# Second layer's MLP in two token groups of 512, and attention of tiles 2 and 3 beside the input projection

## The chip, the core and the metric

The kernel runs on one core of a Trainium2 chip. The metric is the time of one execution in device microseconds (us). The kernel before took 3335.85 us (median of three runs, 3335.21 to 3341.36). The engines: TensorE (PE, matrix products; its weight loads are shown as PEld), VectorE (DVE), ScalarE (ACT), GpSimd (POOL), and SyncE (SP), whose queue issues the DMA transfers here.

## What is computed

A backbone of two layers over 1024 latent tokens and 256 context tokens, each of width 1024. The essential lines of the reference, for one layer and the latent tokens (`h` is the normed and modulated input):

```python
a_z, bq, bk, bv, cq, ck, cv = split_proj(h @ w_in[i])
out_a = chunk_gmlp(a_z, a_ws[i], a_bs[i])                    # chunks of 128 tokens
out_b = window_attn_latent(q_b, k_b, v_b, k_bc, v_bc, b_sink[i])   # window +-128, 8 heads
o_c = diff_attn_latent(q_c, k_c, v_c, k_cc, v_cc, lam)       # 4 heads, two softmax maps, all keys
x = x + g1 * (jnp.concatenate([out_a, out_b, out_c], axis=-1) @ w_out[i])
x = x + g2 * conv_ffn(modulate(rms_norm(x, norm2_g[i]), sh2, sc2),
                      w_up[i], conv_w[i], conv_b[i], w_down[i])
```

`conv_ffn` multiplies by `w_up` (1024 x 5632), convolves each channel over three neighbouring tokens, gates (silu) and multiplies by `w_down` (2816 x 1024). The context tokens pass the first layer in the same way and serve only as keys and values in the second. The output is the latent stream.

## The kernel before

Tokens are worked in tiles of 128: tiles 0 to 7 are latent, 8 and 9 context. All products by weights are made in three terms: `wunit` (L111) loads a block of weights, ScalarE copies its high part (L115) and VectorE or GpSimd subtracts to get the low part (L109), and `mm3` (L123) issues three matmuls for each 128 x 128 block (L130 with the weights stationary, L132 with the tokens stationary).

A layer has these pieces:

- `norms` and `ipset`: norm of each tile, then the input projection in four column blocks, 3 to 0 (`inproj`, L422, matmuls on L132, 512 columns wide). Blocks 3 and 2 hold keys and values and the queries of attention C, block 1 the queries of attention B, block 0 the chunked gating. Results go to scratch memory in DRAM.
- `attn_c(L, hd, groups)` (L785): attention C for one head, over a list of tile pairs. A unit is one head and one pair: it loads the queries; the keys (Kc, L666) and values are loaded once for the head, with the first pair. Scores (L692), maxima on VectorE (L496), exponentials on ScalarE (L695), a combination of both maps on VectorE (L702), transposes (L727), the product with the values (L718), and a short chain that ends with two stores (L775).
- `attn_b(L, tiles)` (L782): attention B for one pair, in two units (one for each key/value head). It ends with four stores a unit (L640).
- `prep(L, G, ...)` (L804): the output projection for the tokens of a group `G` (loads of attention's results, oT, L799; matmuls on L130 that read oT), then the norms of the group's tiles. All columns of the projection, and so all tiles of the group, must be there before the norms.
- `mlp(L, G, ...)` (L840): 22 up steps `up(f)` of two weight blocks each, with the convolution on ScalarE and VectorE (L860 to L867), and down steps `down` after every four or three up steps. A `hook(f)` is called in the middle of up step f; with it the next group's `prep` is placed into the current group's MLP. The numbers in `HK` (L21) say at which step; the loads of oT are issued over the four steps ahead of it.
- `finish(L, G, ...)` (L908): in the second layer it transposes the result (L921) and stores the output.

A group is a run of tokens that share one pass over the MLP's weights: every group loads, splits and multiplies by all of `w_out`, `w_up` and `w_down`. The convolution needs one neighbour on each side, so a group keeps two columns of the one before it. A group's matmuls are as wide as one entry of its `segs` (256, 384, 386, 258 columns); a group with two segments multiplies both by a weight block while it is loaded, but its last down step passes over the weights once for each segment. The first layer has groups of 384 (with the context), 384 and 512 tokens. The second has 256 (tiles 0 and 1), 384 (tiles 2 to 4) and 384 (tiles 5 to 7), L946 to L951.

The engines' instruction order is not the program's order. A planner lays all instructions out by readiness in its own timeline and gives precedence to what stands earlier in the program; so the order of the calls sets precedence, and independent pieces are interleaved. Each engine then runs its list in order, as does SP's queue. What limits interleaving are the buffers of the tile pools. Attention's pool `at` has three key buffers, four for score rows (tag e), three for transposed rows, one for values and one for B's queries, and PSUM has one accumulator O for both attentions. `wide(True)` lets the weight products use two more PSUM banks (zS beside z); while attention runs, it is off.

The order of the second layer's part in question (L1179 to L1223): projection blocks 3 and 2; attention C of pair (0,1) over four heads; block 1; attention B of (0,1); block 0; then, with the projection's pools released, attention B of (2,3) and (4,5); attention C of both; `prep` of group a; attention B and C of (6,7); MLP of group a, with `prep` of group b at step 20; MLP of group b with `prep` of group c at step 12; `wide(True)`; MLP of group c. The `at` pool is released after group a's MLP.

Of the kernel before, what the change touches and what calls it, by code (L numbers as in the profile page):

```python
# [17 lines left out]
DRAM = bass.MemoryType.DRAM  # L18


HK = (16, 13, 20, 12)  # L21

WD = ("dddd", "dddd", "dddd", "dddd")

# [28 lines left out]
def trunk(ctx: ExitStack, tc: tile.TileContext, a: dict):  # L53
    nc = tc.nc
    act, dve, pool, pe, sp = nc.scalar, nc.vector, nc.gpsimd, nc.tensor, nc.sync

    def mkpool(name, bufs, side="left", space=None):
        kw = {"space": space} if space is not None else {}
        return tc.alloc_tile_pool(name=name, bufs=bufs, side=side, reuse_waits="tile", **kw)
# [28 lines left out]
    st = {"wd": 0}  # L88
    wb = {"zs": 4, "sq": 3, "kn": 3, "st": 2}
    xh = const.tile([P, KT], F32, name="xh")  # L90
# [691 lines left out]
    def attn_b(L, tiles, at, mkS, mkT, mkO):  # L782
        attend(units_b(L, tiles, at, mkS, mkT, mkO))

    def attn_c(L, hd, groups, at, mkS, mkT, mkO):  # L785
        attend(units_c(L, hd, groups, at, mkS, mkT, mkO))
# [17 lines left out]
    def prep(L, G, p, mp, pl=None, lo=dve):  # L804

        wd = G["W"]
        xg, oT, loads = pl or prep_loads(L, G, p)
        while loads:
            loads.pop(0)()
        if G["xh"]:  # L810
            dve.tensor_copy(xg[:, :, 0], xh)
        for (xc, n, pieces) in G["op"]:
            for ct in range(KT):
                w = wunit(a["w_out"][L][:, ct * P:ct * P + P], KT, P, eng=lo)
                ps = mkz()
                mm3(ps[:, :n], lambda j, k: w[:, j, k, :], lambda j, k: oT[:, j, k, xc:xc + n], KT)
                for (tok, o, m, s) in pieces:
                    xs = xg[:, ct, xc + o:xc + o + m]
                    sp.dma_start(out=xs, in_=x_s[:, ct, tok:tok + m])
                    dve.scalar_tensor_tensor(out=xs, in0=ps[:, o:o + m], scalar=mods[:, L, 16 + ct, s:s + 1], in1=xs,  # L820
                                             op0=ALU.mult, op1=ALU.add)
        hT = p.tile([P, 2, KT, wd], F32R, tag="h", name="h2", bufs=1)
        if G["xh"]:
            dve.tensor_copy(hT[:, :, :, 0:2], hal.bitcast(F32))
        big = lambda: mp.tile([P, KT, P], F32, name="nb", tag="nb", bufs=2)
        for i, (xc, hc, s) in enumerate(G["norm"]):
            norm_tile(L, 1, xg[:, :, xc:xc + P], s, hT[:, 0, :, hc:hc + P], hT[:, 1, :, hc:hc + P], mkU, big,
                      add=AN[L])

        def halo():  # L830
            if G["halo"] is not None:
                hc, xc = G["halo"]
                dve.tensor_copy(hal, hT[:, :, :, hc:hc + 2].bitcast(F32))
                dve.tensor_copy(xh, xg[:, :, xc])

        return xg, hT, halo
# [71 lines left out]
    def finish(L, G, xg, mp):  # L908
        if L < DEPTH - 1:
            for ct in range(KT):  # L910
                for (tok, xc, n) in G["out"]:
                    sp.dma_start(out=x_s[:, ct, tok:tok + n], in_=xg[:, ct, xc:xc + n])
            return
        for (tok, xc, n) in G["out"]:
            for o in range(0, n, P):
                m = min(P, n - o)
                ot = mp.tile([P, KT, P], F32, name="ot", tag="nb", bufs=2)
                for g in range(2):
                    px = mkT()
                    for k in range(4):  # L920
                        pe.transpose(px[:m, k * P:k * P + P], xg[:, 4 * g + k, xc + o:xc + o + m], ident)  # L921
                    if g:
                        dve.tensor_copy(ot[:m, 4:8], px[:m].rearrange("p (k t) -> p k t", k=4))
                    else:
                        act.activation(out=ot[:m, 0:4], in_=px[:m].rearrange("p (k t) -> p k t", k=4), func=AF.Copy)
                m16 = m - m % 16
                for r0, r1 in ((0, m16), (m16, m)):
                    if r1 > r0:
                        sp.dma_start(out=a["out"][0, tok + o + r0:tok + o + r1, :],
                                     in_=ot[r0:r1].rearrange("p k t -> p (k t)"))  # L930
# [5 lines left out]
    nrm = lambda n: [(1 + 128 * k, 2 + 128 * k, 0) for k in range(n)]  # L936
    G0 = [dict(id="a", xh=False, W=384, op=[(0, 384, [(0, 0, 128, 0), (SEQ, 128, 256, 1)])],
               norm=[(0, 0, 0), (128, 128, 1), (256, 256, 1)], halo=(126, 127),
# [4 lines left out]
          dict(id="c", xh=True, W=514, op=[(1, 512, [(512, 0, 512, 0)])], norm=nrm(4), halo=None,  # L943
               segs=[(0, 258, [(0, 258, 1, 257, 0, 0)]), (256, 258, [(0, 258, 1, 258, 256, 0)])],
               out=[(511, 0, 513)])]
    G1 = [dict(id="a", xh=False, W=256, op=[(0, 256, [(0, 0, 256, 0)])], norm=[(0, 0, 0), (128, 128, 0)],  # L946
               halo=(254, 255), segs=[(0, 256, [(0, 256, 0, 255, 0, 0)])], out=[(0, 0, 255)]),
          dict(id="b", xh=True, W=386, op=[(1, 384, [(256, 0, 384, 0)])], norm=nrm(3), halo=(384, 384),
               segs=[(0, 386, [(0, 386, 1, 385, 0, 0)])], out=[(255, 0, 384)]),
          dict(id="c", xh=True, W=386, op=[(1, 384, [(640, 0, 384, 0)])], norm=nrm(3), halo=None,  # L950
               segs=[(0, 386, [(0, 386, 1, 386, 0, 0)])], out=[(639, 0, 385)])]  # L951
    A1 = [[(2, 3), (4, 5)], [(6, 7)]]


    psA = mkpool("psA", 1, "right", PSUM)
# [15 lines left out]
    def wide(on):  # L971
        zc[1] = on
# [121 lines left out]
    def ahead(L, G, p, f, at_f, key):  # L1094
        if f == at_f - 4:
            st["pl"] = prep_loads(L, G, p)
        if at_f - 4 <= f < at_f:
            st["pl"][2].pop(0)()
        if f == at_f:
            st[key] = prep(L, G, p, M, st["pl"])  # L1100
# [8 lines left out]
    def hook(f):  # L1109
        ahead(0, G0[1], X2, f, HK[0], "x2")  # L1110

# [67 lines left out]
    ipset(1, be, (3, 2), w=w)  # L1179
    wide(False)  # L1180
    for hd in range(4):
        attn_c(1, hd, [(0, 1)], at, mkS, mkT, mkO)
    ipset(1, al[2:] + be, (1,))
    attn_b(1, (0, 1), at, mkS, mkT, mkO)
    ipset(1, al[2:] + be, (0,))
    hp2.release()
    wx.release()
# [1 line left out]
    nwk.release()  # L1189
    hp.release()  # L1190
    M = mkpool("M2", 2, "right")
    X2 = mkpool("X5", 1, "right")
    X1 = mkpool("X4", 1, "right")
    for t in A1[0]:
        attn_b(1, t, at, mkS, mkT, mkO)
    for hd in range(4):
        attn_c(1, hd, A1[0], at, mkS, mkT, mkO)
    x1 = prep(1, G1[0], X1, M)
    for t in A1[1]:
        attn_b(1, t, at, mkS, mkT, mkO)  # L1200
    for hd in range(4):
        attn_c(1, hd, A1[1], at, mkS, mkT, mkO)

    def hook(f):
        ahead(1, G1[1], X2, f, HK[2], "x2")

    mlp(1, G1[0], *x1, M, hook, pool)
    finish(1, G1[0], x1[0], M)
    X1.release()
    at.release()  # L1210
    X3 = mkpool("X6", 1, "left")

    def hook(f):
        ahead(1, G1[2], X3, f, HK[3], "x3")

    mlp(1, G1[1], *st["x2"], M, hook, pool)
    finish(1, G1[1], st["x2"][0], M)
    wide(True)
    mlp(1, G1[2], *st["x3"], M)
    finish(1, G1[2], st["x3"][0], M)  # L1220
    X3.release()
    X2.release()
    M.release()  # L1223
    psD.release()
    psT.release()
# [50 lines left out]
```

## Time and profile before

| what | value |
|---|---|
| time, median of three runs | 3335.85 us (3335.21 to 3341.36) |
| the profiled execution's own time | 3333.47 us |
| its span, first to last instruction | 3331.7 us |
| mean granted clock of TensorE | 0.977 |
| second layer's input projection, last matmul (L132) | 2131.8 us into the span |
| group a: first MLP matmul | 2286.5 us |
| group c: first matmul of the output projection | 2853.6 us |
| last up matmul of the last group | 3307.9 us |

Times within the profile are microseconds from the start of the span, and durations of one instruction are in nanoseconds (ns). A row that groups instructions names the line, engine, operation, the tiles written and read, the shape and the count; behind the bar stand busy time in us, the mean of one instruction in ns, and the idle time of the engine in front of them with what ended it. A row on one line of the kernel has the least, middle and greatest duration, and the first and last start. PEclk is the share of full speed that TensorE was granted.

### The profile page before, as it was taken

Reading aid. Unit: us, or ns where it says so; the run is one execution under the profiler, and the core shown is the slowest. Engines: PE = TensorE matmul, PEld = TensorE weight load, DVE = VectorE, ACT = ScalarE, POOL = GpSimd, SP = SyncE. Lnnn points to the kernel's source line nnn. Section 1 sums busy time; section 2 is a strip of 40 time slices with the busy share of each in tenths; the row PEclk is TensorE's granted clock in tenths of the full one; section 3 lists DMA queues with packets and bytes.
Section 4 is the critical chain, followed back from the end, with each engine's and each line's share of the span. In section 5 each row is a group of like instructions: output and inputs, shape, how many; then the busy total and the mean of one; then the engine's idle time right before and its main releaser. Section 6 shows DMA issues by size and latency. Waiting matters only on the chain.

```text
span 3331.7 us, 54585 instructions
## 1 busy us (share of the span) xinstructions
PE 3152.4 (95%) x19503; PEld 2750.3 (83%) x19503; DVE 2333.3 (70%) x5306; ACT 1744.9 (52%) x3059; POOL 887.0 (27%) x1170
## 2 busy tenths in 40 slices
PE   6999989899999999999999899999999999999999
PEld 3777556787998898998999777766887789999998
DVE  4776756766878785878777678647786685666666
ACT  3555645555556663656444345556665564444443
POOL 1545311223223550138001154222322323222000
PEclk8999989899999999999999999999999999999999
DMA  8655787245442853378343555445555446434433
GB/s 262 194 157 161 227 247 188 81 125 128 128 122 80 258 166 115 101 209 239 88 117 112 161 149 160 143 125 140 161 139 153 123 120 196 122 105 137 136 113 109
DMA packets 754127, 499.52 MB, mean 150 GB/s; under 512 B 81480, under 2 KB 697792, under 8 KB 753856
## 3 DMA queue, kind: packets, MB, share of 16 engines
q1 hardware_dynamic: 753856, 496.03, 52.1%
q8 instruction: 155, 2.54, 0.3%
q14 instruction: 116, 0.95, 0.1%
HBM read 432.48 MB, written 63.44 MB: 149 GB/s over the span
## 4 chain that ended last, share of the span: by engine, by line
PE 70%; DVE 10%; DMA 6%; ACT 3%; issue 3%; POOL 2%; SPq 1%; ACTq 0%; DVEq 0%; POOLq 0%
PE z L130 34%; PE zS L130 11%; PE z L132 7%; PE O L718 3%; PE O L619 3%; PE T L609 2%; PE T L727 2%; DVE wsp L109 2%; PE S L692 2%; DMA raw<-in_w_up_dram 1%; PE zS L132 1%; DVE ec L496 1%; POOL mev L171 1%; DMA mraw<-in_w_ada_dram 1%; DMA raw<-in_w_down_dram 1%
## 5 line engine op out<-in xcount | busy, mean ns | idle before, releaser
L130 PE MATMUL z<-h,wsp 128*128 128x386 f32 (+3 forms) x5280 | 872.9, 319 | 19.8 <-DVE t L867 5.8
L130 PEld LDWEIGHTS z<-h,wsp 128*128 128x128 f32 x5280 | 822.7, 190 | 36.0 <-issue 7.8
L115 ACT ACTIVATE wsp<-raw 128x1024 fp32r<-128x1024 f32 (+2 forms) x660 | 555.9, 845 | 426.9 <-PE z L130 183.8
L109 DVE TENSOR_TENSOR wsp<-raw,wsp 128x1024 fp32r<-128x1024 f32 (+2 forms) x516 | 561.9, 1091 | 104.3 <-ACT wsp L115 101.1
L130 PE MATMUL z<-g,wsp 128*128 128x386 f32 (+3 forms) x2640 | 460.9, 321 | 22.0 <-ACT wsp L115 7.1
L130 PEld LDWEIGHTS z<-g,wsp 128*128 128x128 f32 x2640 | 415.2, 190 | 38.6 <-issue 11.8
L132 PE MATMUL z<-wsp,h 128*128 128x512 f32 x1584 | 405.8, 402 | 14.2 <-ACT h L233 4.8
L109 POOL TENSOR_TENSOR wsp<-raw,wsp 128x128 fp32r<-128x128 f32 x528 | 252.8, 511 | 478.5 <-ACT wsp L115 379.9
L132 PEld LDWEIGHTS z<-wsp,h 128*128 128x128 f32 x1584 | 292.0, 191 | 80.7 <-ACT h L233 5.8
L130 PE MATMUL zS<-h,wsp 128*128 128x386 f32 (+1 forms) x2112 | 332.8, 313 | 5.5 <-DVE t L867 2.4
L130 PEld LDWEIGHTS zS<-h,wsp 128*128 128x128 f32 x2112 | 318.1, 190 | 7.5 <-ACT wsp L115 2.6
L860 ACT ACTIVATE t<-z,cw 128x386 f32<-128x386 f32 (+3 forms) x220 | 137.7, 626 | 220.2 <-PE z L130 219.0
L864 DVE SCALAR_TENSOR_TENSOR t<-z,cw,t 128x255 f32<-128x255 f32 (+3 forms) x264 | 132.7, 503 | 146.2 <-ACT t L860 145.8
L695 ACT ACTIVATE ec<-ec,nmc 128x1280 f32<-128x1280 f32 (+1 forms) x144 | 182.2, 1265 | 54.0 <-DVE ec L496 53.0
L171 POOL TENSOR_TENSOR mev<-mev,mtr 128x512 f32<-128x512 f32 x112 | 175.8, 1582 | 116.1 <-ACT mtr L170 113.1
L130 PE MATMUL z<-oT,wsp 128*128 128x384 f32 (+2 forms) x1056 | 199.4, 335 | 3.9 <-DMA oT<-o_s 2.1
L892 DVE SCALAR_TENSOR_TENSOR xg<-z,mods,xg 128x384 f32<-128x384 f32 (+5 forms) x288 | 140.3, 501 | 86.1 <-PE z L130 85.0
L496 DVE TENSOR_SCALAR_CACHE_REDUCE ec<-S,nmc 128x512 f32<-128x512 f32 (+1 forms) x256 | 156.8, 613 | 57.9 <-PE S L692 54.2
L130 PE MATMUL zS<-g,wsp 128*128 128x386 f32 (+1 forms) x1056 | 180.6, 314 | 9.3 <-DVE wsp L109 2.8
L130 PEld LDWEIGHTS z<-oT,wsp 128*128 128x128 f32 x1056 | 177.0, 188 | 12.7 <-DMA oT<-o_s 3.0
L592 POOL TENSOR_SCALAR dgb<-cst,ls 128x128 f32<-128x128 f32 x144 | 88.9, 631 | 342.5 <-DVE ls L590 175.7
L381 POOL TENSOR_TENSOR rs<-ss,cst 128x8 f32<-128x8 f32 (+1 forms) x76 | 116.6, 1534 | 233.1 <-DVE ss L379 161.2
(248 smaller groups left out, 4853.6 us busy)
## 6 DMA issues: line engine op xcount, KB each, us to landing
raw<-in_w_up_dram SPq DMA_DIRECT2D x264, 512.0 KB
mraw<-in_w_ada_dram SPq DMA_DIRECT2D x96, 512.0 KB
raw<-in_w_down_dram SPq DMA_DIRECT2D x192, 256.0 KB
Kc<-qk_s SPq DMA_DIRECT2D x96, 320.0 KB
raw<-in_w_in_dram SPq DMA_DIRECT2D x52, 512.0 KB
raw<-in_w_out_dram SPq DMA_DIRECT2D x48, 512.0 KB
raw<-in_w_down_dram SPq DMA_DIRECT2D x104, 192.0 KB
qk_s<-st SPq DMA_DIRECT2D x18, 512.0 KB
```

Of the source, the lines that this page charges most:

```text
L109: eng.tensor_tensor(out=lo, in0=src, in1=hi.bitcast(F32), op=ALU.subtract)
L115: act.activation(out=hl[:, 0], in_=raw, func=AF.Copy)
L130: pe.matmul(ps, w(i, k), h(j, k), start=s, stop=e)
L132: pe.matmul(ps, h(i, k), w(j, k), start=s, stop=e)
L171: pool.tensor_tensor(out=acc[s], in0=acc[s], in1=pr, op=ALU.add)
L381: pool.tensor_tensor(out=rs[:, :ns], in0=ss[:, 1, :ns], in1=mhalf[:, :ns], op=ALU.pow)
L496: dve.tensor_scalar(out=neg, in0=s_ap, scalar1=-1.0, scalar2=init, op0=ALU.mult, op1=ALU.min, accum_out=acc)
L619: pe.matmul(po[64 * ti:64 * ti + 64, 256 * hp:256 * hp + 256], V[:, ix[pk], 64 * g:64 * g + 64], pPT[:, 256 * m:256 * m + 256], start=(pk ...
L695: act.activation(out=e[:, :nk], in_=e[:, :nk], func=AF.Exp, scale=-1.0, bias=acc, accum_out=l1[:, m, ti:ti + 1])
L860: act.activation(out=t[:, o:o + n], in_=ps[:, :n], func=AF.Identity, scale=cw[:, L, 1, ft:ft + 1], bias=cw[:, L, 3, ft:ft + 1])
L864: dve.scalar_tensor_tensor(out=t[:, o + b + 1:o + e], in0=ps[:, b:e - 1], scalar=cw[:, L, 0, ft:ft + 1], in1=t[:, o + b + 1:o + e], op0=AL ...
L892: dve.scalar_tensor_tensor(out=xs, in0=ps[:, b + o0:b + o1], scalar=mods[:, L, 40 + ct, s:s + 1], in1=xs, op0=ALU.mult, op1=ALU.add)
```

## The change

In the second layer the groups become two, each of 512 tokens: tiles 0 to 3 with one segment of 512 columns, and tiles 4 to 7 with two segments of 258. Attention C and B of pair (2,3) are called together with those of (0,1), among the input projection's blocks. Attention B of (4,5) stands ahead of `prep` of group a; attention B of (6,7) and attention C of (4,5) and (6,7), which share a key load, stand behind it. Group b is prepared within the MLP of group a, at step 18; its pool is placed at step 14, where attention's pool `at` is released in the same call. `wide(True)` comes ahead of the MLP of group b. The first layer is as it was.

```diff
-HK = (16, 13, 20, 12)
+HK = (16, 13, 18)
...
-    G1 = [dict(id="a", xh=False, W=256, op=[(0, 256, [(0, 0, 256, 0)])], norm=[(0, 0, 0), (128, 128, 0)],
-               halo=(254, 255), segs=[(0, 256, [(0, 256, 0, 255, 0, 0)])], out=[(0, 0, 255)]),
-          dict(id="b", xh=True, W=386, op=[(1, 384, [(256, 0, 384, 0)])], norm=nrm(3), halo=(384, 384),
-               segs=[(0, 386, [(0, 386, 1, 385, 0, 0)])], out=[(255, 0, 384)]),
-          dict(id="c", xh=True, W=386, op=[(1, 384, [(640, 0, 384, 0)])], norm=nrm(3), halo=None,
-               segs=[(0, 386, [(0, 386, 1, 386, 0, 0)])], out=[(639, 0, 385)])]
-    A1 = [[(2, 3), (4, 5)], [(6, 7)]]
+    G1 = [dict(id="a", xh=False, W=512, op=[(0, 512, [(0, 0, 512, 0)])], norm=[(128 * k, 128 * k, 0) for k in range(4)],
+               halo=(510, 511), segs=[(0, 512, [(0, 512, 0, 511, 0, 0)])], out=[(0, 0, 511)]),
+          dict(id="b", xh=True, W=514, op=[(1, 512, [(512, 0, 512, 0)])], norm=nrm(4), halo=None,
+               segs=[(0, 258, [(0, 258, 1, 257, 0, 0)]), (256, 258, [(0, 258, 1, 258, 256, 0)])],
+               out=[(511, 0, 513)])]
...
     for hd in range(4):
-        attn_c(1, hd, [(0, 1)], at, mkS, mkT, mkO)
+        attn_c(1, hd, [(0, 1), (2, 3)], at, mkS, mkT, mkO)
     ipset(1, al[2:] + be, (1,))
-    attn_b(1, (0, 1), at, mkS, mkT, mkO)
+    for t in ((0, 1), (2, 3)):
+        attn_b(1, t, at, mkS, mkT, mkO)
     ipset(1, al[2:] + be, (0,))
...
-    X2 = mkpool("X5", 1, "right")
     X1 = mkpool("X4", 1, "right")
-    for t in A1[0]:
-        attn_b(1, t, at, mkS, mkT, mkO)
+    attn_b(1, (4, 5), at, mkS, mkT, mkO)
+    x1 = prep(1, G1[0], X1, M)
+    attn_b(1, (6, 7), at, mkS, mkT, mkO)
     for hd in range(4):
-        attn_c(1, hd, A1[0], at, mkS, mkT, mkO)
-    x1 = prep(1, G1[0], X1, M)
-    for t in A1[1]:
-        attn_b(1, t, at, mkS, mkT, mkO)
-    for hd in range(4):
-        attn_c(1, hd, A1[1], at, mkS, mkT, mkO)
+        attn_c(1, hd, [(4, 5), (6, 7)], at, mkS, mkT, mkO)
 
     def hook(f):
-        ahead(1, G1[1], X2, f, HK[2], "x2")
+        if f == HK[2] - 4:
+            at.release()
+            st["X"] = mkpool("X5", 1, "left")
+        if f >= HK[2] - 4:
+            ahead(1, G1[1], st["X"], f, HK[2], "x2")
 
     mlp(1, G1[0], *x1, M, hook, pool)
     finish(1, G1[0], x1[0], M)
+    wide(True)
+    mlp(1, G1[1], *st["x2"], M)
+    finish(1, G1[1], st["x2"][0], M)
+    st["X"].release()
     X1.release()
...
```

The lines left out at the end remove the third group's `mlp`, `finish` and pools.

More of the change, by code (lines that the diff above doesn't have):

```diff
@@ L1191, in trunk @@
     M = mkpool("M2", 2, "right")
-    X2 = mkpool("X5", 1, "right")
     X1 = mkpool("X4", 1, "right")
-    for t in A1[0]:
-        attn_b(1, t, at, mkS, mkT, mkO)
+    attn_b(1, (4, 5), at, mkS, mkT, mkO)
+    x1 = prep(1, G1[0], X1, M)
+    attn_b(1, (6, 7), at, mkS, mkT, mkO)
     for hd in range(4):
-        attn_c(1, hd, A1[0], at, mkS, mkT, mkO)
-    x1 = prep(1, G1[0], X1, M)
-    for t in A1[1]:
-        attn_b(1, t, at, mkS, mkT, mkO)
-    for hd in range(4):
-        attn_c(1, hd, A1[1], at, mkS, mkT, mkO)
-    def hook(f):
-        ahead(1, G1[1], X2, f, HK[2], "x2")
+        attn_c(1, hd, [(4, 5), (6, 7)], at, mkS, mkT, mkO)
+    def hook(f):
+        if f == HK[2] - 4:
[3 more added lines that the diff above has]
+            ahead(1, G1[1], st["X"], f, HK[2], "x2")
     mlp(1, G1[0], *x1, M, hook, pool)
     finish(1, G1[0], x1[0], M)
+    wide(True)
+    mlp(1, G1[1], *st["x2"], M)
+    finish(1, G1[1], st["x2"][0], M)
+    st["X"].release()
     X1.release()
[L1210 to L1222, printed above, removed]
     M.release()
```

## The prediction

> **What bounds the kernel now.** I read the page first, then busy time by stages, then the first and last instruction of each piece of the second layer.
>
> ```profile
> span 3331.7 us, 54585 instructions
> PE 3152.4 (95%) x19503; PEld 2750.3 (83%) x19503; DVE 2333.3 (70%) x5306; ACT 1744.9 (52%) x3059; POOL 887.0 (27%) x1170
> PE 70%; DVE 10%; DMA 6%; ACT 3%; issue 3%; POOL 2%; SPq 1%; ACTq 0%; DVEq 0%; POOLq 0%
> ```
>
> TensorE (PE) holds 70% of the chain of waits; VectorE (DVE) comes next. "95% busy" hides losses, because matmuls overlap and a waiting stream still looks busy. So I count matmuls against time, stage by stage. Columns: window, its length, each engine's busy time with its instructions, granted clock, DMA share, GB/s.
>
> ```profile
> core 0: us, PE busy (x) PEld busy (x) DVE busy (x) ACT busy (x) POOL busy (x), PEclk, DMA share, GB/s
> 1994.00:2132.00 138.00, 135.67 (x745) 105.97 (x743) 110.35 (x306) 75.57 (x143) 50.53 (x55) 0.99 0.47 129
> 2132.00:2286.00 154.00, 138.26 (x943) 96.18 (x943) 85.53 (x318) 92.26 (x187) 44.24 (x59) 0.94 0.54 155
> 2286.00:2533.00 247.00, 232.91 (x1832) 205.69 (x1831) 195.35 (x481) 156.59 (x275) 68.70 (x136) 0.98 0.55 151
> ...
> 3060.00:3308.00 248.00, 248.00 (x1398) 247.77 (x1397) 169.71 (x258) 107.50 (x158) 0.00 (x0) 1.00 0.42 120
> ...
> 560.00:606.00 46.00, 31.96 (x153) 20.86 (x152) 36.32 (x105) 33.48 (x63) 9.15 (x6) 0.70 0.52 130
> ...
> 1600.00:1700.00 100.00, 100.00 (x835) 100.00 (x834) 68.06 (x117) 41.25 (x61) 0.00 (x0) 1.00 0.38 110
> ```
>
> The last MLP (3060 to 3308) is pure TensorE: 1398 matmuls in 248 us, 177 ns each at 386 columns. First layer, third group: 835 in 100 us, 120 ns each at 258 columns. Two stretches of the chain give the other widths:
>
> ```profile
> 1293.66 5.58 PE z L130 x24
> ...
> 2482.06 5.71 PE z L130 x48
> ```
>
> That is 232.5 ns at 512 columns and 119 ns at 256. With these the same stage rows, restricted to the MLP's line L130, show what everything else takes from TensorE's stream:
>
> ```profile
> 2286.00:2533.00 247.00, 167.52 (x1242) 156.88 (x1243) 0.98 0.55 151
> 2760.00:3060.00 300.00, 290.09 (x1605) 281.89 (x1606) 1.00 0.49 145
> 3308.00:3332.00 24.00, 13.91 (x73) 12.09 (x71) 0.94 0.25 91
> 830.00:1085.00 255.00, 193.83 (x1006) 174.36 (x1006) 1.00 0.41 110
> ```
>
> ```profile
> L775 SPq DMA_DIRECT2D o_s<-stc x16: 602/607/1212, 2358.6 to 2574.1; - x16
> ...
> L775 SPq DMA_DIRECT2D o_s<-stc x16: 580/607/1526, 870.3 to 1116.7; - x16
> ```
>
> These are the stores of attention C around the first and the last of those windows, two for each unit (a head times a tile pair): eight units each. From 2286 to 2533 the 1242 narrow matmuls account for 148 us, so 99 us went to attention C of tiles 2 to 5 and its stalls: eight units, 12.4 us each. In the first layer, beside 384-column matmuls at 177 ns, 255 - 178 = 77 us bought eight: 9.6 us each. A change of group (output projection, norms, finish) cost 300 - 284 = 16 us (2760 to 3060), the end behind the last matmuls 24 - 13 = 11 us.
>
> The order of the pieces, by first and last start:
>
> ```profile
> L132 PE MATMUL z<-wsp,h x408: 387/394/628, 1981.6 to 2131.8; 128*128 128x512 f32 x136
> ...
> L130 PE MATMUL z<-oT,wsp x192: 276/279/384, 2137.4 to 2252.6; 128*128 128x256 f32 x192
> ...
> L130 PE MATMUL z<-h,wsp x240: 276/280/562, 2286.5 to 2336.0; 128*128 128x256 f32 x120
> ...
> L775 SPq DMA_DIRECT2D o_s<-stc x6: 607/608/1964, 2058.0 to 2121.7; - x6
> ...
> L640 SPq DMA_DIRECT2D o_s<-stb x24: 575/612/883, 2167.4 to 2309.8; - x24
> ```
>
> The input projection ends at 2132, the MLP of group a begins at 2286, and in the 154 us between them TensorE has only attention B and 192 narrow projection matmuls. Two C intervals from 2058 to 2122 make a pace of 31 us beside the projection. A B unit (half an attn_b) stores four times: 24 stores from 2167 to 2310 are six units, about 27.6 us apart.
>
> **The change, part by part.** *MLP and output projection.* Each group has 1056 up, 528 down and 192 projection matmuls. Before: 1776 x 119 ns + 2 x 1776 x 177 ns = 840 us. After: 1776 x 232.5 ns for group a = 413 us; for group b 192 x 232.5 ns = 45 us and 2 x 1584 x 120 ns = 380 us; together 838 us. Fewer groups save TensorE nothing worth naming. What goes is weights: 44 up units, 8 output units and a net 40 down units (144 to 104, since the last down step of a two-segment group loads its weights twice), each a load on SP, a ScalarE copy and a subtraction. All of that lies beside matmuls, so its own price is zero; it counts only through the pace of attention. Without this cover one up unit would cost 2.3 us, a copy and a subtraction:
>
> ```profile
> L109 DVE TENSOR_TENSOR wsp<-raw,wsp 128x1024 fp32r<-128x1024 f32 x364 | 452.6, 1244 | 93.4 <-ACT wsp L115 91.8 <-issue 0.8
> ...
> L115 ACT ACTIVATE wsp<-raw 128x1024 fp32r<-128x1024 f32 x364 | 383.1, 1054 | 243.7 <-PE z L130 92.0 <-DMA raw<-in_w_up_dram 76.2 <-DMA raw<-in_w_in_dram 35.2
> ```
>
> *Attention C beside a wider MLP.* Its own VectorE work, 2286 to 2533:
>
> ```profile
> L702 DVE SCALAR_TENSOR_TENSOR ec<-ec,rho 128x1280 f32<-128x1280 f32 x16 | 25.2, 1578 | 0.2
> L496 DVE TENSOR_SCALAR_CACHE_REDUCE ec<-S,nmc 128x512 f32<-128x512 f32 x32 | 23.9, 746 | 1.1 <-PE S L692 0.8
> L496 DVE TENSOR_SCALAR_CACHE_REDUCE ec<-S 128x512 f32<-128x512 f32 x32 | 21.9, 685 | 11.4 <-PE T L609 6.1 <-PE S L692 3.0 <-PE T L727 2.2
> ...
> L496 DVE TENSOR_SCALAR_CACHE_REDUCE ec<-S,nmc 128x256 f32<-128x256 f32 x32 | 15.3, 479 | 11.4 <-PE S L692 11.0
> ```
>
> The four groups sum to 86.3 us, 10.8 us a unit. A weight split takes 1.24 us against 24 x 119 ns = 2.9 us of narrow matmuls, and against 5.6 us of wide ones, so beside 512 columns VectorE has more room. The two prices seen are 12.4 (256 columns) and 9.6 (384); for 512 I take 9.0, nearest to the second. Bounds 7 and 12.4.
>
> *The stretch in front of the MLP.* Attention C and B of tiles 2 and 3 move ahead of the output projection, with all they issue: on SP eight query loads of C, the B loads of keys, values and queries, and the stores. Key and value loads of C are shared by two pairs, so those of one pair per head vanish. SP works in order, so weight loads of the projection stand behind these; the projection left 0.47 of DMA in that window and I charge nothing. By 2132 about four of eight C units are through at 31 us, and no projection matmul is left. The other four stand alone. First-layer rows for attention without dense matmuls:
>
> ```profile
> L775 SPq DMA_DIRECT2D o_s<-stc x6: 607/608/608, 448.9 to 492.1; - x6
> ...
> L640 SPq DMA_DIRECT2D o_s<-stb x16: 574/612/1262, 304.8 to 374.3; - x16
> ```
>
> C: two intervals in some 42 us, 21 each; B: three in about 67 us, 22.5 each. C cannot go below its 10.8 us of VectorE. I take 17, between them and nearer the pace seen, because a shared key load takes one wait out of every second unit: 4 x 17 = 68 us (bounds 43 and 84). For B, four units at 25, between 22.5 and 27.6: 100 us (90 to 110). Only then can projection a start: it now needs tiles 0 to 3. It runs beside attn_b(4,5); the first layer did 192 matmuls of 384 columns beside one attn_b thus:
>
> ```profile
> L130 PE MATMUL z<-oT,wsp x192: 331/338/450, 494.5 to 559.3; 128*128 128x384 f32 x192
> ...
> L130 PE MATMUL z<-h,wsp x116: 332/338/687, 606.0 to 640.0; 128*128 128x384 f32 x116
> ```
>
> 65 us there, and 192 x (232.5 - 177) ns = 10 us more here: 75 (bounds 66, 86). From there to the first MLP matmul 46 us (three tiles normed; two tiles took 2252.6 to 2286.5, 34 us); four tiles with attn_b(6,7) as filler, 46 (34 to 60). Sum 68 + 100 + 75 + 46 = 289 us where 154 stood: MLP a begins at 2132 + 289 = 2421.
>
> *From there to the end.* Matmuls 368 (1584 x 232.5 ns) + 45 + 380 = 793; eight C units of tiles 4 to 7 at 9.0 = 72; one change of group, four tiles for three, 16 x 4/3 = 21; the end 11. Together 897, so the span ends at 2421 + 897 = 3318. The same arithmetic on the kernel before (188 + 629 matmuls, twelve units at 12.4 = 149, two changes 32, the end 11) gives 1009 of the 1045 us behind 2286.5 and leaves 36 for attn_b(6,7), 18 a unit, which is plausible beside filler.
>
> So two thirds of a gain are paid back: 149 us less behind the MLP's start, 135 us more ahead of it, 14 us won. The profiled execution took 3333.47 us with a span of 3331.7; the median of the runs is 3335.85, 4 above the span. 3318 + 4 gives **3322 us**.
>
> *The memory release.* The pool of group b is now placed where attention's tiles lie, at up step 14 of 22. Its loads wait for the last attention instruction, and behind them on SP wait the weight loads. Eight units at (9.0 + a wide share) 30 to 35 us end at 2660 to 2700; step 14 falls near 2421 + 14/22 x 368 + 8 x 9 = 2727. I price it at nothing; each us beyond that slack would be a us of weights late, first hidden by three buffers.
>
> **The rivals.**
>
> *Bare attention costs more than it returns (slower).* Place: from the last input projection matmul to the first of MLP a. If units without filler go at 26 us, halfway between 21 and 31, four of them take 104, not 68: 3322 + 36 = 3358 us. It decides from 20.4 us a unit on (17 + 14/4). For it: in 560 to 606 attention stood almost alone, TensorE was busy 32 of 46 us and its granted clock was 0.70; 2132 to 2286 shows 0.94. Against it: 448.9 to 492.1 at 21 us, beside slow modulation loads.
>
> [...]
>
> *The mixing is even (faster).* If the planner spreads eight C units over the projection so that VectorE is the limit: 110 us are busy in 138 with four units; four more add 43, 153 us, at the same 80% 192 us from 1994, ending at 2186. That is 54 for 68: 3308 us; with the C price at 7 (16 less) 3292.
>
> *The two sides cancel (no change).* If a C unit beside 512 columns still costs 10.8, its bare VectorE time, 14 us are added: 3336. For it: 9.6 against 12.4 may come from the first layer's clock (1.00 against 0.98) or fuller fillers, not from width. That the planner, which orders by readiness, leaves C of tiles 2 and 3 behind the projection anyway ends here too.
>
> *Late release or an unchanged price of 12.4:* 8 x 3.4 = 27 us, 3349.
>
> **How the numbers follow.** Forecast 0.40, even mixing 0.12, cancelling 0.18, bare attention 0.22, late release or price 0.08. About 0.2% (6.7 us) is what a measurement of this kernel tells from no change. Faster: 0.40 + 0.12 = 0.52; within 0.18; slower 0.22 + 0.08 = 0.30. The bounds of the terms (C alone -25/+16, B 10 each way, projection a 10, norms 13, C price -16/+27), taken as independent, give about 35 each way; the range 3282 to 3362 reaches both outer rivals. The forecast's own range is 3300 to 3335.
>
> **What would show it.** In the changed profile: the first MLP matmul near 2421 (later than 2440 speaks for bare attention); a stretch behind the last L132 matmul with two C stores about 17 us apart; L130 matmuls at 232 ns with C units at 9 us beside them; 120 ns to the end; no gap on L130 near up step 14. The forecast is wrong if MLP a starts after 2435 or if the wide matmuls lose as much to attention as the narrow ones did.

## The result: slower by half a per cent

| kernel | median | runs | ratio to before, 95% interval |
|---|---|---|---|
| before | 3335.53 us | 3332.84 to 3341.78 | |
| changed | 3357.17 us | 3349.0 to 3364.08 | 1.0057 [1.0042, 1.0071] |

The change costs 21.6 us of median. The forecast was 3322 us, inside a range of 3282 to 3362; the time landed, in part by luck as shown below, on the rival called "bare attention costs more than it returns" (3358 us). The profiled execution of the changed kernel took 3364.08 us, the highest of its runs, so its stretches are read one by one and its whole is not.

The page of the changed kernel's profile, its first line and the busy time of each engine:

```profile
span 3362.1 us, 53442 instructions
...
PE 3176.0 (94%) x19311; PEld 2670.7 (79%) x19311; DVE 2281.1 (68%) x5184; ACT 1669.7 (50%) x2923; POOL 803.6 (24%) x994
```

There are 1143 instructions fewer than before (54585), 192 of them matmuls, and VectorE, ScalarE and GpSimd are busy for less (2281 against 2333, 1670 against 1745, 804 against 887 us). Still the span is longer. Less work and more time is a loss in the order or the waits, so the next view is the second layer's pieces, by first and last start:

```profile
L132 PE MATMUL z<-wsp,h x429: 387/393/795, 1979.8 to 2136.2; 128*128 128x512 f32 x143
...
L775 SPq DMA_DIRECT2D o_s<-stc x4: 608/608/1750, 2066.3 to 2106.7; - x4
...
L775 SPq DMA_DIRECT2D o_s<-stc x12: 602/608/622, 2139.1 to 2237.2; - x12
...
L640 SPq DMA_DIRECT2D o_s<-stb x32: 574/611/791, 2256.2 to 2456.9; - x32
...
L130 PE MATMUL z<-oT,wsp x180: 387/393/505, 2318.0 to 2399.6; 128*128 128x512 f32 x180
...
L130 PE MATMUL z<-h,wsp x50: 387/395/796, 2459.6 to 2479.9; 128*128 128x512 f32 x50
```

The input projection ends at 2136. Group a's first MLP matmul moves from 2286.5 to 2459.6. Between them stand, one after the other, attention C (to 2237), attention B (to 2329), the output projection (to 2400; the row counts from 2200 on, and 12 of its 192 matmuls ran before that, from 2178.6) and the norms. The second and third row count C's stores ahead of 2137 and behind it. Each unit ends with two stores, 0.6 us apart: two C units have stored before the projection ends, a third stores just behind it, and five more follow up to 2237.2, (2237.2 - 0.6 - 2139.1)/5 = 19.5 us apart (the first three at 21, then 18.6 and 16.1).

The same stretch in windows (columns as in the prediction's table of windows):

```profile
core 0: us, PE busy (x) PEld busy (x) DVE busy (x) ACT busy (x) POOL busy (x), PEclk, DMA share, GB/s
1994.00:2136.60 142.60, 139.01 (x730) 109.05 (x729) 114.41 (x298) 75.36 (x134) 56.12 (x55) 0.98 0.45 124
2136.60:2237.80 101.20, 80.71 (x455) 56.19 (x453) 67.07 (x231) 53.41 (x110) 12.73 (x18) 0.79 0.37 110
2237.80:2328.60 90.80, 82.23 (x515) 49.87 (x514) 38.16 (x173) 50.74 (x107) 21.55 (x32) 0.94 0.35 98
2328.60:2400.00 71.40, 70.33 (x381) 47.90 (x380) 26.91 (x76) 29.40 (x53) 9.68 (x14) 1.00 0.43 124
2400.00:2459.60 59.60, 49.60 (x275) 28.75 (x274) 48.44 (x166) 45.55 (x91) 21.39 (x25) 0.90 0.32 84
2459.60:2788.50 328.90, 328.86 (x1664) 257.47 (x1665) 219.97 (x438) 159.40 (x258) 63.96 (x113) 0.99 0.32 88
3033.00:3329.00 296.00, 296.00 (x2469) 296.00 (x2468) 192.19 (x329) 112.45 (x171) 0.00 (x0) 1.00 0.32 92
```

From 2136.6 to 2237.8 no engine is full: TensorE is shown busy for 81 of 101 us, at a granted clock of 0.79; VectorE is busy for 67, ScalarE for 53. That looks like a chain of dependent steps with little beside it. Four of the waits in this window (from 2140 to 2236) show its links:

```profile
ACT PT L729 <- PE T L727: 20.3, 18, 3.8
PEld S L692 <- DVE ec L496: 14.0, 21, 2.4
ACT ec L695 <- DVE ec L496: 9.7, 9, 2.5
DVE ec L496 <- PE S L692: 9.2, 7, 4.1
```

ScalarE's copies wait for TensorE's transposes (20 us), the next score matmuls wait for VectorE to release their bank (14 us), the exponentials wait for VectorE's maxima and those again for scores. With little other work in the window such waits can end up on the path. The profile's chain of waits does not reach back to this window, so how much each costs is not shown.

Restricted to the MLP's matmuls, the row of the wide stretch:

```profile
2459.60:2788.50 328.90, 270.73 (x1095) 203.73 (x1096) 0.99 0.32 88
```

1095 x 232.5 ns = 254.6 us, so 74.3 us went to the eight C units of tiles 4 to 7 that lie in it: 9.3 us each.

### The profile page after: what moved, and what is told of

Read it like the earlier page. It is cut to its first block, busy times and chain, and to the rows that moved or that the text cites. A ratio compares the mean times of both kernels' runs of the same rounds, so it can differ in the third digit from the quotient of the medians.

```text
span 3362.1 us, 53442 instructions
## 1 busy us (share of the span) xinstructions
PE 3176.0 (94%) x19311; PEld 2670.7 (79%) x19311; DVE 2281.1 (68%) x5184; ACT 1669.7 (50%) x2923; POOL 803.6 (24%) x994
## 5 line engine op out<-in xcount | busy, mean ns | idle before, releaser
L130 PE MATMUL z<-h,wsp 128*128 128x258 f32 (+3 forms) x4752 | 838.3, 329 | 7.6 <-DVE t L867 2.6
L130 PE MATMUL z<-g,wsp 128*128 128x258 f32 (+3 forms) x2376 | 441.0, 333 | 24.0 <-ACT wsp L115 8.0
L130 PE MATMUL zS<-h,wsp 128*128 128x258 f32 (+1 forms) x2640 | 370.4, 295 | 8.4 <-ACT wsp L115 3.0
L860 ACT ACTIVATE t<-z,cw 128x258 f32<-128x258 f32 (+3 forms) x198 | 127.8, 646 | 267.8 <-PE z L130 267.6
L864 DVE SCALAR_TENSOR_TENSOR t<-z,cw,t 128x127 f32<-128x127 f32 (+3 forms) x242 | 125.0, 517 | 189.8 <-ACT t L860 189.6
L130 PE MATMUL zS<-g,wsp 128*128 128x258 f32 (+1 forms) x1320 | 202.6, 298 | 10.2 <-ACT g L877 3.2
L892 DVE SCALAR_TENSOR_TENSOR xg<-z,mods,xg 128x257 f32<-128x257 f32 (+4 forms) x264 | 132.3, 516 | 98.9 <-PE z L130 97.6
L130 PE MATMUL z<-oT,wsp 128*128 128x512 f32 (+1 forms) x864 | 195.2, 375 | 2.0 <-DMA oT<-o_s 2.0
L130 PEld LDWEIGHTS zS<-g,wsp 128*128 128x128 f32 x1320 | 183.0, 191 | 15.3 <-ACT wsp L115 4.8
L692 PE MATMUL S<-Kc,qc 128*128 128x512 f32 (+1 forms) x400 | 160.5, 423 | 27.2 <-DVE ec L496 24.2
```

The lines of the kernel that those rows point to most:

```text
L130: pe.matmul(ps, w(i, k), h(j, k), start=s, stop=e)
L692: pe.matmul(S[:, :w_], q[:, m, ti * P:ti * P + P], K[m][:, o:o + w_], start=True, stop=True)
L860: act.activation(out=t[:, o:o + n], in_=ps[:, :n], func=AF.Identity, scale=cw[:, L, 1, ft:ft + 1], bias=cw[:, L, 3, ft:ft + 1])
L864: dve.scalar_tensor_tensor(out=t[:, o + b + 1:o + e], in0=ps[:, b:e - 1], scalar=cw[:, L, 0, ft:ft + 1], in1=t[:, o + b + 1:o + e], op0=AL ...
L892: dve.scalar_tensor_tensor(out=xs, in0=ps[:, b + o0:b + o1], scalar=mods[:, L, 40 + ct, s:s + 1], in1=xs, op0=ALU.mult, op1=ALU.add)
```

## The experiments

Theory A has two parts: C units without dense matmuls beside them cost more (the bare stretch), and the need makes it so, since group a's one output projection needs the attention of all four tiles, so that the stretch runs out of dense matmuls whatever the order. Its rivals place the loss in the move, in the order of the units, or behind the MLP's start; each expectation names what it tests. From one profile to another the second layer's first C exponential falls anywhere from 1994.3 to 2005.5 us, so pieces are compared from that point ("from C's start").

### The two halves of the change, each alone

`move_only`: the three groups of before, with attention of (2,3) moved.

```diff
-    A1 = [[(2, 3), (4, 5)], [(6, 7)]]
+    A1 = [[(4, 5)], [(6, 7)]]
...
-        attn_c(1, hd, [(0, 1)], at, mkS, mkT, mkO)
+        attn_c(1, hd, [(0, 1), (2, 3)], at, mkS, mkT, mkO)
...
-    attn_b(1, (0, 1), at, mkS, mkT, mkO)
+    for t in ((0, 1), (2, 3)):
+        attn_b(1, t, at, mkS, mkT, mkO)
```

> The three groups of before, with attention of tiles 2 and 3 moved among the projection's blocks as in the change. Theory A (bare stretch: behind the last projection matmul the moved attention has no matmuls beside it, four more C units at 20 us where they cost 12.4 beside the narrow MLP): C(2,3) +30 us, given back in part because the output projection and MLP of tiles 0 and 1 need only pair (0,1) and fill B(2,3) and B(4,5): 3340 to 3355 us. Rival B (not the move but the four-tile group is to blame): 3330 to 3338 us, as before.

`groups_only`: the two groups of the change, with attention of (2,3) left behind the input projection.

```diff
-        attn_c(1, hd, [(0, 1), (2, 3)], at, mkS, mkT, mkO)
+        attn_c(1, hd, [(0, 1)], at, mkS, mkT, mkO)
...
-    for t in ((0, 1), (2, 3)):
-        attn_b(1, t, at, mkS, mkT, mkO)
+    attn_b(1, (0, 1), at, mkS, mkT, mkO)
...
+    attn_b(1, (2, 3), at, mkS, mkT, mkO)
+    for hd in range(4):
+        attn_c(1, hd, [(2, 3)], at, mkS, mkT, mkO)
     attn_b(1, (4, 5), at, mkS, mkT, mkO)
```

> Two groups of 512, but attention of tiles 2 and 3 left behind the projection (B, then C, then B of (4,5), then the output projection). Theory A: tiles 0 to 3 are needed before any MLP matmul, so the same eight C units and the same B units stand in front of it with the same filler: 3350 to 3365 us, like the change. Rival C (the place is to blame: the moved attention crowds the projection): 3320 to 3338 us.

Measured: `move_only` 3360.2 us, 1.0067 [1.0045, 1.0089]; `groups_only` 3336.05 us, 0.9993 [0.9981, 1.0005]. The moved attention alone, with the old narrow groups, costs what the whole change costs; the new groups alone cost and bring nothing. Both sides missed on the first (more was lost than either gave), and the second part of theory A fell on the second: there group a needs the same four tiles and has the same single projection, and nothing is lost. From C's start to group a's first MLP matmul it took 436 us, in the change 454 (457 when it was run again), and from there to the end 901.4 against 902.5. So the loss lies in front of the MLP and comes from where, and in what order, the moved units stand.

### What the moved units cost in each place

Attention C of (2,3) in the second layer left out (its stores are made from (0,1)'s result, so that as many bytes move), in the change, in the kernel before and in `groups_only`; the diff shows the call in the change:

```diff
-        attn_c(1, hd, [(0, 1), (2, 3)], at, mkS, mkT, mkO)
+        attn_c(1, hd, [(0, 1)], at, mkS, mkT, mkO)
```

> The change without attention C of pair (2,3) in the second layer (the result of pair (0,1) is stored in its place as well). Theory A: the four units cost their bare price of 20 us, 78 us less, 3279 us (3270 to 3290). Rival (the price beside matmuls, 9.3 us a unit, and the loss lies elsewhere): 37 us less, 3320 us.

> The kernel before without attention C of pair (2,3) in the second layer (the result of pair (0,1) is stored in its place). Both theories: four units at the price beside narrow matmuls, 12.4 us, 50 us less: 3286 us (3278 to 3296). The difference to after_no_c23 gives the price of the same four units in the two places.

> groups_only without attention C of (2,3) in the second layer (the result of pair (0,1) is stored in its place as well). If the units cost their price of the place behind the projection: 3336 - 4 x 17 = 3267 us, the same as the change without them, since the two then differ only in where B(2,3) stands: 3260 to 3274 us. If B(2,3) ahead of the last block is part of the loss: 3250 to 3260 us.

Measured: 3267.01 us, 0.9804 [0.9790, 0.9819]; 3292.54 us, 0.9885 [0.9868, 0.9901]; 3271.51 us, 0.9802 [0.9788, 0.9815]. The first lies just under the lower bound of theory A, the other two within theirs. The four units' price is the difference of ratios to the same kernel before, times 3336 us:

| place of C of (2,3) | working | price | a unit |
|---|---|---|---|
| before: beside the narrow MLP | 1 - 0.9885 | 38 us | 9.6 us |
| `groups_only`: behind attention B | 0.9993 - 0.9802 | 64 us | 16 us |
| the change: in a row with (0,1) | 1.0057 - 0.9804 | 84 us | 21 us |

In `groups_only` the price holds a key load for each head as well, which in the other two the units share with another pair. Without these units the change is 0.9885 - 0.9804 = 0.0081 faster than the kernel before, 27 us; with them it pays 84 - 38 = 46 us more; 46 - 27 = 19 us is its loss of 0.0057. This sum follows from the four ratios and is no further test. It says that the new groups gain where these four units are left out (`groups_only` too, 0.9885 - 0.9802), and that the dearer place of the units eats the gain. So the first part of theory A holds: the price of the same units follows what stands beside them.

In `groups_only` the four units stand as bare as in the change, behind attention B:

```profile
2236.00:2312.00 76.00, 60.04 (x353) 41.35 (x353) 48.13 (x163) 39.89 (x80) 7.59 (x12) 0.84 0.44 121
```

But they are four and not five, and their stores come 17.4 us apart and not 19.5: 76 us for 101.

### The order of the units

`reorder_only`: the change, with C of (0,1), B of (0,1), C of (2,3), B of (2,3) in this order; groups, projection and place as in the change, which ran beside it again as `after_again`.

```diff
-        attn_c(1, hd, [(0, 1), (2, 3)], at, mkS, mkT, mkO)
+        attn_c(1, hd, [(0, 1)], at, mkS, mkT, mkO)
...
-    for t in ((0, 1), (2, 3)):
-        attn_b(1, t, at, mkS, mkT, mkO)
+    attn_b(1, (0, 1), at, mkS, mkT, mkO)
+    for hd in range(4):
+        attn_c(1, hd, [(2, 3)], at, mkS, mkT, mkO)
+    attn_b(1, (2, 3), at, mkS, mkT, mkO)
```

> The change, with both attentions of (0,1) ahead of both of (2,3) among the projection's blocks (keys of C loaded once more per head); the output projection is not split. Order theory (eight C units in a row are what is dear: C leaves TensorE emptier than B, and B(0,1) loses the projection's tail as its filler): 3330 to 3342 us, as groups_only. Place theory (any attention of (2,3) ahead of the last projection block is dear): 3350 to 3362 us, as the change.

> The change as it is, for a second profile beside the others: in the first one the first layer, whose instructions are the same, was already 11 us late. 3350 to 3362 us; in the profile some 455 us from the second layer's first C exponential to the first MLP matmul, and some 902 us from there to the end.

Measured: 3336.4 us, 0.9993 [0.9983, 1.0003], against 3357.07 us, 1.0057 [1.0044, 1.0069]. That is inside the order theory's range. The order alone is worth 20.7 us, the change's whole loss, although the keys of C are loaded once more per head. Attention's windows in `reorder_only`, from the last projection matmul to the last attention store, and then its norms:

```profile
2132.60:2189.40 56.80, 49.86 (x303) 31.94 (x302) 36.71 (x135) 34.21 (x73) 14.61 (x20) 0.94 0.68 195
2189.40:2265.00 75.60, 59.49 (x342) 40.94 (x342) 47.88 (x161) 40.23 (x81) 7.57 (x12) 0.75 0.39 105
2265.00:2307.80 42.80, 41.01 (x272) 25.32 (x270) 19.41 (x85) 25.61 (x52) 9.61 (x14) 1.00 0.39 112
2378.70:2432.80 54.10, 45.05 (x270) 27.70 (x269) 43.52 (x156) 43.12 (x86) 20.41 (x25) 0.97 0.31 79
```

and its stores of C up to the projection's end, behind it, and of B:

```profile
L775 SPq DMA_DIRECT2D o_s<-stc x6: 607/608/1822, 2059.5 to 2122.1; - x6
...
L775 SPq DMA_DIRECT2D o_s<-stc x6: 602/607/608, 2147.2 to 2228.6; - x6
...
L640 SPq DMA_DIRECT2D o_s<-stb x16: 577/612/1356, 2166.7 to 2307.2; - x16
```

The second row ends at 2245; two more units store up to 2264. Three C units have stored by 2122, and the first B store comes at 2167, where the change's comes at 2256. B's first score matmul (L568) runs at 2109.6, while the projection lasts, and in the change at 2209.6: B takes part in the projection's cover and runs between the C units, at clocks of 0.94 and 1.00; what remains of bare C is four units in 76 us (0.75) where it was five in 101. The three attention windows sum to 175 us, the change's two to 192. Against `after_again`, from C's start, 13.3 of the 20 us are won by the last attention store (311.8 for 325.1) and 6.7 in the norms (54.1 us for 60.8).

### The projection in two halves

`split_prep`: group a's output projection in two halves of 256 columns, so that the first needs only tiles 0 and 1; the MLP stays 512 wide. `split_reorder`: this and the order of `reorder_only`. `split_behind`: this in `groups_only`.

```diff
-    G1 = [dict(id="a", xh=False, W=512, op=[(0, 512, [(0, 0, 512, 0)])], ...
+    G1 = [dict(id="a", xh=False, W=512, op=[(0, 256, [(0, 0, 256, 0)]), (256, 256, [(256, 0, 256, 0)])], ...
```

> The change, with the output projection of group a in two column halves of 256 (tiles 0 and 1, then 2 and 3; w_out passed twice). TensorE work is the same (2 x 192 x 119 ns = 46 us for 45). Theory A: the first half, 23 us, and the norms of two tiles move into the bare stretch: 15 to 40 us less than the change, 3317 to 3342 us. Rival D (TensorE's stream is not idle there, attention's own chain fills it): within 8 us of the change, 3350 to 3365 us.

> As split_prep, and in addition both attentions of (0,1) come ahead of both of (2,3), keys of C loaded once more per head. The first half of the output projection can then run beside C(2,3), where the profile of the change has TensorE idle most (51 of 101 us without work). Theory A: 0 to 12 us less than split_prep, 3310 to 3335 us. Rival D: as the change, 3350 to 3365 us.

> Attention of (2,3) behind the projection as in groups_only, and the output projection of group a in two halves as in split_prep. If the half that needs only tiles 0 and 1 is worth the same here as in the change (19 us): 3313 to 3322 us. If it was already beside something in groups_only: 3328 to 3338 us.

Measured: 3338.53 us, 1.0002 [0.9992, 1.0011]; 3325.52 us, 0.9959 [0.9945, 0.9974]; 3329.79 us, 0.9982 [0.9967, 0.9997]. By the ratios the split takes 18 us from the change, 11 from the reordered change and 4, which the intervals hardly tell from none, from `groups_only`. The first two times lie in theory A's ranges for the bare stretch, the third in the range for a half that had work beside it already. The split helps most where most is lost: the 192 matmuls of the first half can run before attention of tiles 2 and 3 is through (in `split_prep` they begin, but for 12, 260 us behind C's start; the change's begin, but for 12, at 312). The windows of `split_reorder`, from C's start to the last projection matmul, to the first of the MLP, and from there to 2740:

```profile
1999.50:2133.00 133.50, 131.23 (x731) 102.39 (x729) 107.15 (x295) 72.89 (x137) 50.37 (x54) 1.00 0.47 128
2133.00:2418.50 285.50, 253.02 (x1694) 177.64 (x1693) 179.03 (x606) 173.50 (x338) 65.74 (x83) 0.93 0.52 143
2418.50:2740.00 321.50, 321.18 (x1629) 248.83 (x1628) 226.88 (x461) 162.75 (x262) 58.34 (x107) 1.00 0.34 93
```

The stretch between the projection and the MLP takes 285.5 us where the change's four windows sum to 323. This kernel is faster than before by 0.4%, and faster than the change by 1.0%. `split_behind`, in which attention of (2,3) is not moved, comes to 0.9982 in the same way. What the move itself adds, 8 us by the ratios, is hardly shown, since the two intervals overlap.

### Is there room for more matmuls?

192 matmuls of 512 columns (192 x 232.5 ns = 45 us) added behind the last projection block, once in the change and once in the kernel before; their results are not used.

```diff
-    ipset(1, al[2:] + be, (0,))
+    wl = ipset(1, al[2:] + be, (0,))
+    for i in al[2:] + be:
+        z = mkz()
+        mm3(z, lambda j, k: wl[k // 2][:, j, k % 2, :], lambda j, k: hts[i][:, j, k, :], KT, stat_w=False)
```

> The change with the last projection block's matmuls of tiles 0 to 7 issued a second time behind it (192 matmuls of 512 columns, 44 us of TensorE, no result read). Theory A: they fall into the bare stretch, where TensorE lacks work for some 115 us: 0 to 15 us more than the change, 3357 to 3372 us. Rival D (the stream is full there): 44 us more, 3401 us. If the low clock of that stretch (0.79) is what costs, the filler keeps it up and the time falls, to 3340 to 3355 us.

> The kernel before with the same 192 matmuls issued a second time at the same place. Its stretch from 2132 to 2286 holds some 46 us without TensorE work, mostly in pieces: 10 to 30 us more, 3345 to 3366 us. Rival D: 44 us more, 3380 us.

Measured: 3370.39 us, 1.0114 [1.0099, 1.0129]; 3350.14 us, 1.0058 [1.0043, 1.0073]. In both the 45 us cost 19 (1.0114 - 1.0057 and 1.0058 - 1, times 3336); the other 26 run where TensorE stood. In the change the matmuls keep the projection going until 2189. From C's start, the last C store comes 28 us later than without them (259 us for 232), and the first MLP matmul 20 us later (474 for 454). What remains of bare attention runs at this:

```profile
2188.60:2268.00 79.40, 64.76 (x379) 43.87 (x378) 42.14 (x161) 39.33 (x85) 9.08 (x15) 0.83 0.38 118
```

So there are some 26 us in the change that matmuls can use, but as many in the kernel before: room alone does not tell them apart. The time that a kept-up clock was expected to save in the change (3340 to 3355 us) did not come.

### Clock or chain? (inconclusive)

Is C bare slow because the clock falls, or because its chain through VectorE and ScalarE has nothing beside it? 96 matmuls of 512 columns, their results unused, were put behind score rows: in the change for heads 2 and 3, and in `split_reorder` for pair (2,3).

```diff
+                        if L == 1 and tiles[0] < 4 and hd >= 2:
+                            z = mkz()
+                            for _ in range(6):
+                                pe.matmul(z, q[:, m, ti * P:ti * P + P], K[m][:, 0:512], start=True, stop=True)
```

Half clock is what the trace of the change shows in part of its bare stretch: the granted clock is 0.50 from 2152 to 2162 and from 2176 to 2184, and 1.00 from 2164 to 2172 and from 2186 to 2194. As an estimate, with each window's mean clock taken as a mix of these two, the time at half clock between the last projection matmul and the first of the MLP is 2 x (0.22 x 102.1 + 0.07 x 91.9 + 0.13 x 60.8) = 74 us in `after_again` and 2 x (0.06 x 56.8 + 0.25 x 75.6 + 0.03 x 54.1) = 48 us in `reorder_only`. What makes the clock fall is not shown.

> The change, with six matmuls of 512 columns, whose result is not read, behind each score row of the four C units of heads 2 and 3 of pairs (0,1) and (2,3): 96 matmuls, 22 us of TensorE at full clock, within the bare stretch. Clock theory (TensorE at half clock for 73 us between the last projection matmul and the first MLP matmul of the change, 48 us in reorder_only, is what the longer bare stretch adds to its idleness): half-clock time falls and the kernel takes 5 to 15 us less than the change, 3342 to 3352 us. Chain theory (the units are bound by their own order of VectorE and ScalarE, and the clock matters little): 0 to 15 us more than the change, 3357 to 3372 us.

> split_reorder, with the same six matmuls behind each score row of the four C units of pair (2,3). Clock theory: 3 to 10 us less than split_reorder, 3315 to 3323 us. Chain theory: 0 to 15 us more, 3325 to 3341 us.

Measured: 3369.31 us, 1.0105 [1.009, 1.012]; 3364.27 us, 1.0088 [1.007, 1.0106]. The first lies in the chain theory's range, the second in neither. The trace shows that the edit did something else as well. The projection's matmuls in `after_warm`, and the same row's busy time inside one window:

```profile
L132 PE MATMUL z<-wsp,h x444: 387/393/499, 1959.8 to 2252.3; 128*128 128x512 f32 x148
...
1990.00:2111.00 121.00, 0.00 (x0) 0.00 (x0) 0.82 0.32 87
```

There is not one projection matmul from 1990 to 2111, where the change had them all along: the added matmuls take the projection's own PSUM banks (z), and those projection matmuls that stand later in the calls came behind them. In `split_reorder_warm` the same happens from 2050 to 2214. Both kernels therefore had attention without projection matmuls at another place, and neither tells what a warmer clock is worth. The question stays open.

## Why the prediction was wrong

**The forecast failed at one step,** in the stretch in front of the MLP: "By 2132 about four of eight C units are through at 31 us, and no projection matmul is left. The other four stand alone. ... 4 x 17 = 68 us". Measured: two have stored and a third is at its end, five stand alone, at 19.5 us; from the projection's end to the last C store 101 us. That is 33 us more. The two halves of the error were a count and a pace. The count: the row that gave the pace of 31 us shows three units stored by 2122, and in the kernel before the fourth stored at 2148, behind the projection, so "about four" was one too many from the start. C beside the projection did not speed up when twice as many units were offered: from C's start the third unit stored at 134 us (127 before), and the projection ended at 131 (138 before). The pace: 19.5, nearer the 21 us of the quoted first-layer row than the 17 taken. Where only four units stood bare, in `groups_only` and `reorder_only`, they went at 17.4 and 17.9 and took 76 us. The step's bounds of 43 and 84 us did not hold it, because they bounded the pace and not the number of units.

**The second miss is the norms:** "four tiles with attn_b(6,7) as filler, 46 (34 to 60)". They took 59.6, the end of the bounds. The norm's sums (VectorE, L222) of the four tiles:

```profile
L222 DVE TENSOR_TENSOR nb<-xg,U x4: 1215/1216/1222, 2413.5 to 2453.9; 128x1024 f32<-128x1024 f32 x4
```

They come (2453.9 - 2413.5)/3 = 13.5 us apart, one tile after the other. The order of attention matters here too (54.1 us in `reorder_only`).

**What held.** Attention B of four units 91 us (100 predicted; its first matmuls ran beside C), the projection 71 (75). No gain from TensorE in the MLP: 3033 to 3329 shows 296 us for 2469 matmuls, 120 ns each. C beside the wide MLP 9.3 us a unit (9.0). From the first MLP matmul to the end 902.5 us (897). The release of attention's pool at step 14 cost next to nothing, but with less slack than thought: the last C store came at 2788, not by 2700, group b's loads of oT went out right behind it, at 2789, and its projection, at step 18, began at 2833. The TensorE waits recorded from 2690 to 2840 come to 2.7 us. So the sum was made of the right terms: stretch 289 against 323 us, rest 897 against 902.5, and the projection's end 5 us later than before. Those three, 34, 5.5 and 5 us, are the 44 us between the span of 3318 and the 3362.1 of this profile; the second layer's C began 11 us later in this execution (first exponential at 2005.5 against 1994.3), so the last of the three belongs to that: from C's start the projection ended earlier than before.

**What held only as a sum.** The price of 12.4 us for a C unit beside the narrow MLP was not that high: leaving four of them out of the kernel before saved 9.6 us each (8.3 to 11.0 by the interval). The window behind the 12.4 also held the end of the last B unit, which stored at 2307. So no fall of C's price from narrow to wide matmuls (9.6 to 9.3) is shown, though the time from the first MLP matmul to the end came out. And 135 of 149 us paid back, the prediction's own figures, are nine tenths and not two thirds: its gain of 14 us was a small difference of large sums.

**The rivals.** Bare attention came true in place and in size, though by its own terms it should not have: it was to decide from 20.4 us a unit on, and the pace stayed just under that. The fifth unit made up for it. Its price of 3358 came from four units at 26, which no run shows: that the time agrees is luck. The granted clock was 0.79 in the bare stretch, a mean of 1.00 and 0.50 by turns (0.75 in that of `reorder_only`), so the bare units did not run at half clock throughout. Whether that clock is what makes a bare unit dear is what the two inconclusive runs were to tell, and it is not shown. Even mixing fell: the planner did not spread eight units over the projection. Of the cancelling rival one half came true, that C units stay behind the projection (five of eight), but not its outcome. That a C unit beside 512 columns costs its VectorE time fell (9.3 against 10.8). The late release fell.

**What the prediction never considered** is the order within the moved work. It priced the place of the eight C units as given; the runs show that the list "all C, then all B" in the calls is worth 20.7 us, all that lies between the change and no change, and that with it mended the forecast's gain is still not there (0.9993). Only with the projection cut as well does it pay (0.9959), and with the new groups, the cut and the attention left in its place it is 0.9982, which the intervals do not tell from that.

## What to carry to other kernels

Work with long dependent chains is not free because it is moved early: price it by what stands beside it in the new place, and count how many units get through before the dense work ends, since here the same four units cost 38, 64 or 84 us. A wider group saves work but waits for more; here it helped to cut the step that gathers it (the projection) so that half of it is ready early, and to alternate the kinds of attention rather than queue one kind behind the other. When a change does two things, run each alone first: two runs showed here that one half, the move, made the whole loss.

## What was not expected of the hardware

Between profiles of kernels with the same first layer, the point at which the second layer's first C exponential runs moved by up to 11 us (1994.3 to 2005.5), and by 6 us between two profiles of the changed kernel (1999.8 and 2005.5); so profiles of single executions had to be compared by stretches; why it moves is open. The row of the last stores of the first layer, in the kernel before:

```profile
L912 SPq DMA_DIRECT2D x_s<-xg x8: 319/468/1599, 1861.9 to 1873.4; - x8
```

and in the changed kernel, 9 to 12 us later with no call changed ahead of it:

```profile
L912 SPq DMA_DIRECT2D x_s<-xg x8: 319/338/1281, 1871.3 to 1885.4; - x8
```

A granted clock of 0.75 to 0.79 over 76 to 101 us, with TensorE shown busy for four fifths of it, had only a rival's place in the forecast; with 45 us of added matmuls it was 0.83 in what was left, and the time did not fall (1.0114 for 1.0057). What it costs by itself no run here separates.
